# Two dense steps moved behind the corner products, and next block's keys released from the gate pair, in a hybrid RWKV-7 / short-convolution step

## The chip, the core and the metric

The kernel runs on one core of a Trainium2 chip, in one launch. The metric is the device time of that launch in microseconds (us). TensorE is PE in the profile (its weight loads are PEld), VectorE is DVE, ScalarE is ACT, GpSimd is POOL, and SP is the queue that issues nearly all the transfers. Each engine works through its own instructions in the order in which they stand in the program, and waits for others by semaphores.

## The reference

One layer of a diffusion backbone on 384 tokens (128 of a prompt, 256 of a sample), D = 2048. What matters here:

```python
z = h @ w_in                                   # one wide projection
zs = token_shift(z[..., :N_SHIFTED])           # r, k, v, low-rank decay and rate inputs
g_a, b_gate, c_gate, x_b, g_b, m_a, m_b = split(z[..., N_SHIFTED:])
decay = exp(-exp(-softplus(-w_lin) - 0.5)); a = sigmoid(...)
kk = k * k_k; kk = kk / max(norm(kk per head), 1e-12)
k_dir = k * (1 + (a - 1) * k_a)
# scan over tokens, both directions, 32 heads of 64:
S = S * w_t + (S @ (-kk_t)) outer (kk_t * a_t) + v_t outer k_t;  y = S @ r_t
y_a = (groupnorm(y) + bonus) * silu(g_a) @ w_out_a
y_b = (b_gate * conv3(c_gate * x_b) * silu(g_b)) @ w_out_b
out = x + gate * ((sigmoid(m_a) * y_a + sigmoid(m_b) * y_b) @ w_o)
```

Everything is float32. A dense product is made of three products of rounded parts (high by high, high by low, low by high).

## The kernel before

**Dense stream.** The wide projections are a stream of pairs: a pair is two output tiles of 128 columns, contracted over 2048, in 32 *dense steps* of three matmuls (L81, L82, L83) of 128x384. Its weights come in two halves; each half is loaded (`raw`), then split in two quarters by ACT (`whi`, L88) and DVE (`wlo`, L89). There are two `raw` buffers, and three each of `whi` and `wlo`. A generator gives out one dense step at a time: `ds_.go(n)` puts n of them on PE. TensorE's order is this written order; the other engines' order is set by a scheduler at build time from its own estimate and from priorities (the scan has a higher one).

**Scans.** 16 blocks of 128 channels (two heads) run one after the other, and their short products are put between dense steps. A block b runs:

- `prep_b`: scaled keys, the products `pA` (L695), masked into `A` by DVE (L701) for two directions. The 32x32 triangles on the diagonal of `A` are inverted on DVE: a chain of 60 small operations on `U` (L716, L718), ahead of it a trip through DRAM (`ui`), behind it a copy of the transpose on ACT (`UT`, L722), a second trip through DRAM (`uo`), and loads into `A` and `x11` (called x in the profile).
- `prep_c`: transposes, `pav`, the state.
- `prep_a(b + 1)`: the **keys of the next block**. Four low-rank products `pl` (weights `lraw`, split into `lwh` on ACT and `lwl` on DVE), a norm product `pn` (L633, L634), and then the key rows on DVE: `kn` (L636, three reciprocals L638, L639), `L` (L646), `kd` (L651, L652), `sig` (L653); the scheduler also puts rows of the next `prep_b` and `prep_c` behind them (`bk` L667 and L668, L775, L776).
- `scan`: the two **corner products** `pH` and `pX` (L843), each with four copies from PSUM, two on ACT and two on DVE in turn (L849 into x, L863 into `A`), three dense steps and the product `po` between them (with its addition L806 on DVE), then the **first solve** `pq` (L822), and the two chains of solves and state updates.

Block b needs its own rk pair (`rk{b}`: r and k) before `prep_a(b)`; the pair `gv{b}` gives block b's output gate and block b+1's v. At the start of each block the pairs `rk{b+1}` and `gv{b}` are put at the head of the stream; three filling pairs (tags ma, mb, bc, bx, bg, gb) follow. The dense steps between the parts are a table of numbers: H0 = 3 after `pH` and after `po`, H1 = 4 after `pX`, WINDOW = 80 from the end of `prep_b` to the scan.

The driver lets `prep_a(b + 1)` begin once `gv{b}` is done, and then fills up to the window. In blocks 2 to 14 the pair ends so late that `prep_a` stands directly ahead of `pH`, and the 80 steps are exceeded (84).

Of the kernel before, what the change touches and what calls it, by code (L numbers as in the profile page):

```python
# [20 lines left out]
NB = 16  # L21
# [35 lines left out]
def hybrid_step(ctx, tc, cst, x_prompt, x_sample, state_f, state_b, c, c_ctx, ada_w, ada_b, norm_g,  # L57
# [22 lines left out]
    def mm3(out, wh, wl, xh, xl, start, stop):  # L80
        TE.matmul(out, wh, xh, start=start, stop=False)  # L81
        TE.matmul(out, wh, xl, start=False, stop=False)  # L82
        TE.matmul(out, wl, xh, start=False, stop=stop)  # L83

    def split(src, shape, th, tl, pool, nm, rows=P):
        hi = pool.tile(shape, F32R, tag=th, name=f"{th}_{nm}")
        lo = pool.tile(shape, F32R, tag=tl, name=f"{tl}_{nm}")
        S.copy(hi[0:rows], src)  # L88
        V.tensor_tensor(lo[0:rows], src, hi[0:rows].bitcast(F32), ALU.subtract)  # L89
        return hi, lo  # L90


    PB0, PB1, H0, H1, CH0, CH1 = 14, 6, 3, 4, 2, 4
    PRO, WINDOW, FIRST, LAST = 32, 80, 24, 16

    def wload(view, k0, cols, nm):

# [84 lines left out]
    ds_ = Stream()  # L182
# [70 lines left out]
    def pcol(i, n=1):  # L253
        return par[:, i:i + n]
# [146 lines left out]
    r_, k_, v_, ga_ = {}, {}, {}, {}  # L401
    box = {}

    def tmp(nm):
        return box["sp"].tile([P, T], F32, tag="t", name=nm, bufs=8)
# [184 lines left out]
    def bank(nm):  # L590
        return ps1.tile([P, 4, P], F32, tag="A", name=nm, bufs=5)

    def c3(a):
        return a.rearrange("p (n t) -> p n t", t=C)

    def flat(a):
        return a.rearrange("p n t -> p (n t)")
# [4 lines left out]
    def hl_parts(t, hi, nm):  # L602
        lo = sp.tile([P, T], F32R, tag="t", name=f"lo_{nm}", bufs=8)
        S.copy(hi[:], t[:])
        V.tensor_tensor(lo[:], t[:], hi[:].bitcast(F32), ALU.subtract)
        return hi, lo

    def prep_a(b, o):

        bs = slice(b * P, (b + 1) * P)  # L610
        r, k, v = r_[b], k_[b], v_[b]
        kk = sp.tile([P, T], F32, tag="kk", name=f"kk_{b}")
        S.mul(kk[:], k[:], pcol(KK + b))
        sq = tmp(f"sq_{b}")
        S.activation(sq[:], kk[:], AF.Square)
        sqh, sql = hl_parts(sq, sp.tile([P, T], F32R, tag="hl", name=f"sqh_{b}"), f"sq_{b}")
        sig = []
        for m in range(4):
            if m % 2 == 0:
                lraw = sp.tile([96, 2, P], F32, tag="lraw", name=f"lraw_{b}_{m}")  # L620
                nc.sync.dma_start(lraw[:], (w2, a2)[m // 2][0][:, :, bs].rearrange("d r n -> r d n"))
                lwh, lwl = split(lraw[:], [96, 2, P], "lwh", "lwl", sp, f"{b}_{m}", rows=96)
                yield 2
            pl = bank(f"pl_{b}_{m}")
            pl = flat(pl[:, 0:3, :])
            mm3(pl, lwh[:, m % 2, :], lwl[:, m % 2, :], l_hi[:, m, :], l_lo[:, m, :], True, True)
            t = tmp(f"sig_{b}_{m}")
            S.activation(t[:], pl, AF.Sigmoid, bias=pcol((W0, W0 + 16, A0, A0 + 16)[m] + b))
            sig.append(t)
            yield 2  # L630
        pn = bank(f"pn_{b}")
        pn = flat(pn[:, 0:3, :])
        TE.matmul(pn, bones_r[:], sqh[:], start=True, stop=False)  # L633
        TE.matmul(pn, bones_r[:], sql[:], start=False, stop=True)  # L634
        kn = sp.tile([P, T], F32, tag="kn", name=f"kn_{b}")
        V.tensor_scalar(kn[:], pn, 1e-24, None, ALU.max)  # L636
        for q in range(3):
            V.reciprocal(kn[:, q * P:(q + 1) * P], kn[:, q * P:(q + 1) * P])  # L638
        V.scalar_tensor_tensor(kn[:], kk[:], -1.0, kn[:], ALU.mult, ALU.mult)  # L639
        o.update(kk=kk, ep=[], em=[], kd=[], bn=[])  # L640
        for d in range(2):
            def nat(a):
                return a[:, ::-1] if d else a[:]
            sg, aa = sig[d], sig[2 + d]
            L = tmp(f"L_{b}_{d}")
            V.tensor_tensor_scan(L[:], segm, sg[:], 0.0, op0=ALU.mult, op1=ALU.add)  # L646
            ep = eps_[b % 2, d]
            S.activation(ep[:, :, 1:C + 1], c3(L[:]), AF.Exp, scale=-DECAY)
            S.activation(sg[:], L[:], AF.Exp, scale=DECAY)
            kd = tmp(f"kd_{b}_{d}")  # L650
            V.tensor_scalar(kd[:], aa[:], pcol(KA + b), omka[:, b:b + 1], ALU.mult, ALU.add)  # L651
            V.tensor_tensor(kd[:], nat(k), kd[:], ALU.mult)  # L652
            V.tensor_tensor(aa[:], nat(kn), aa[:], ALU.mult)  # L653
            o["ep"].append(ep)
            o["em"].append(sg)
            o["kd"].append(kd)
            o["bn"].append(aa)
# [238 lines left out]
    def norm(b, o):  # L896

        ytok = o["ytok"]
        y6 = ytok[:].rearrange("p q (h i) -> p (q h) i", i=C)
        mu = sp.tile([P, 6], F32, tag="mu", name=f"mu_{b}")  # L900
        V.tensor_reduce(mu[:], y6, AX.X, ALU.add)
        V.tensor_scalar(mu[:], mu[:], 1.0 / C, None, ALU.mult)
        V.tensor_tensor(y6, y6, mu[:].unsqueeze(2).broadcast_to([P, 6, C]), ALU.subtract)
        sq = tmp(f"ysq_{b}")
        S.activation(sq[:], flat(ytok[:]), AF.Square)
        var = sp.tile([P, 6], F32, tag="var", name=f"var_{b}")
        V.tensor_reduce(var[:], sq[:].rearrange("p (q i) -> p q i", i=C), AX.X, ALU.add)
        V.tensor_scalar(var[:], var[:], 1.0 / C, GN_EPS, ALU.mult, ALU.add)  # L908
        rs = sp.tile([P, 6], F32, tag="rs", name=f"rs_{b}")
        G.tensor_tensor(rs[:], var[:], nhalf[:], ALU.pow)  # L910
        V.tensor_tensor(y6, y6, rs[:].unsqueeze(2).broadcast_to([P, 6, C]), ALU.mult)

    def finish(b, o):

        py = bank(f"py_{b}")
        for q in range(3):
            TE.transpose(py[:, q, :], o["ytok"][:, q, :], ident)
        ya = tmp(f"ya_{b}")
        S.activation(ya[:], flat(py[:, 0:3, :]), AF.Identity, scale=pcol(LG + b), bias=pcol(LB + b))
        V.tensor_tensor(ya[:], ya[:], o["bon"][:], ALU.add)  # L920
        V.tensor_tensor(ya[:], ya[:], ga_[b][:], ALU.mult)
        nc.sync.dma_start(ya_d[b], ya[:])

    def drive(gen, prio=0):
        n = 0
        while True:
            with tc.high_priority(offset=prio):
                u = next(gen, None)
            if u is None:
                return n  # L930
            ds_.go(u)
            n += u

    ds_.go(PRO)
    cur = {}
    drive(prep_a(0, cur))
    prev = None
    for b in range(NB):
        if b < NB - 1:
            if b > 0:  # L940
                ds_.urgent += [(add_rk, b + 1), (add_gv, b)]
        if b == NB - 2:
            ds_.fills += [(add_gv, NB - 1)] + [(add_ob, g) for g in range(8)]
        pb_gen = prep_b(b, cur)
        ds_.go(next(pb_gen))
        if prev is not None:
            finish(b - 1, prev)
        drive(pb_gen)
        n = drive(prep_c(b, cur))
        nxt = {}  # L950
        if b < NB - 1:
            while f"gv{b}" not in ds_.done:
                ds_.go(1)
                n += 1
            n += drive(prep_a(b + 1, nxt))
        w = WINDOW + (FIRST if b == 0 else LAST if b == NB - 1 else 0)
        if n < w:
            ds_.go(w - n)
        drive(scan(b, cur), 300)
        norm(b, cur)  # L960
        prev, cur = cur, nxt
# [97 lines left out]
    for nq in range(3):  # L1059
# [8 lines left out]
        for q in range(4):  # L1068
            raw = wp.tile([P, 4, 512], F32, tag="raw", name=f"raw_wo{nq}_{q}", bufs=2)
            nc.sync.dma_start(raw[:], wov[:, 4 * q:4 * q + 4, ns])  # L1070
            for e in range(2):
                hi, lo = split(raw[:, 2 * e:2 * e + 2, :], [P, 2, 512], "whi", "wlo", wp, f"wo{nq}_{q}_{e}")
                for s in range(3):
                    tsl = slice(s * P, (s + 1) * P)
                    for kk in range(2):
                        k = 4 * q + 2 * e + kk
# [7 lines left out]
    for half in range(2):  # L1084
# [8 lines left out]
        for s in range(3):  # L1093
# [10 lines left out]
            if half == 1:  # L1104
                f = rsf[:, s, :]
# [37 lines left out]
```

## Time and profile before

| what | value |
|---|---|
| time, median of 3 runs (lowest, highest) | 2264.56 us (2261.35, 2266.23) |
| the profiled execution: time, span | 2259.46 us, 2257.7 us |
| granted TensorE clock | 0.996 |
| busy: PE, DVE, ACT, POOL | 2187.7 us (97%), 1522.4 (67%), 1048.9 (46%), 118.6 (5%) |
| matmuls | 16084 |
| one block of the scans | about 106 us |

The time counts the launch as a whole, the span runs from the first instruction to the last; 1.8 us lie between them. A busy share is a mean over parts of the program with different limits. In the chain of work that ended last PE has 90%.

In the profile's rows, `x48` is a count, `out<-in` names tiles without their buffer numbers, a number in brackets is the idle time of that engine just before the row, with what ended it; "issue" means that the profile does not show what did.

### The profile page before, as it was taken

To read this page: it belongs to the slowest core of one execution; us is meant where nothing else is said; L and a number is where in the kernel's file an instruction comes from. 1 tells how busy PE (TensorE), PEld (TensorE's weight loads), DVE (VectorE), ACT (ScalarE), POOL (GpSimd) and SP (SyncE) were. 2 spreads that over 40 slices of the span, in tenths; PEclk is the share of its full clock that TensorE was granted. 3 is DMA by queue.
4 is the path that set the end of the run, shared out by engine and by line. 5 is a ranking of instruction groups with operands and counts; after the bars stand their busy time and mean duration, and the time that the engine had idled before them with its cause. 6 is when DMAs were issued, how large, how long until landed. Compare 5 with 4: busy or idle time off the path is not lost.

```text
span 2257.7 us, 40435 instructions
## 1 busy us (share of the span) xinstructions
PE 2187.7 (97%) x16084; PEld 2072.2 (92%) x16084; DVE 1522.4 (67%) x3096; ACT 1048.9 (46%) x1852; POOL 118.6 (5%) x115
## 2 busy tenths in 40 slices
PE   5999999999999999999999999999999999999998
PEld 3588999999999999999999999999999899889988
DVE  3249567777777778776878687777767774444444
ACT  4246445454545455454545454545455543333233
POOL 2001010101010100000010101010100000000000
PEclk9999999999999999999999999999999999999999
DMA  9963544444444444353444444444445465985633
GB/s 334 347 203 116 147 137 126 114 121 114 110 132 112 125 116 126 105 132 102 122 108 132 111 112 127 113 115 141 121 118 143 133 187 161 309 299 190 219 131 113
DMA packets 429646, 339.97 MB, mean 151 GB/s; under 512 B 84801, under 2 KB 411025, under 8 KB 428561
## 3 DMA queue, kind: packets, MB, share of 16 engines
q1 hardware_dynamic: 427968, 335.62, 50.6%
q8 instruction: 127, 2.08, 0.4%
q10 hardware_dynamic: 432, 1.57, 0.2%
q14 instruction: 63, 0.51, 0.1%
q0 software_dynamic: 1056, 0.19, 0.1%
HBM read 307.37 MB, written 29.36 MB: 149 GB/s over the span
## 4 chain that ended last, share of the span: by engine, by line
PE 90%; DMA 5%; DVE 2%; issue 2%; SPq 1%; ACT 1%; POOLq 0%; POOL 0%; DVEq 0%; ACTq 0%
PE d_rk L81 4%; PE d_gv L81 4%; PE d_gv L83 4%; PE d_gv L82 4%; PE d_rk L83 4%; PE d_rk L82 4%; DMA raw_adah<-in_ada_w_dram 3%; PE d_oa L81 2%; PE d_bx L81 2%; PE d_bg L81 2%; PE d_bc L81 2%; PE d_mb L81 2%; PE pq L822 2%; PE d_bg L83 2%; PE d_bg L82 2%; PE d_bx L83 2%
## 5 line engine op out<-in xcount | busy, mean ns | idle before, releaser
L716 DVE TENSOR_TENSOR ut<-U 48x30 f32<-48x30 f32 (+14 forms) x480 | 154.6, 322 | 16.2 <-DMA U<-ui 4.2
L81 PE MATMUL d_rk<-h_hi,whi_rk 128*128 128x384 f32 x480 | 164.3, 342 | 0.6 <-ACT lst L549 0.6
L718 DVE TENSOR_TENSOR U<-U,ut 48x30 f32<-48x30 f32 (+14 forms) x480 | 154.3, 321 | 10.8
L81 PE MATMUL d_gv<-h_hi,whi_gv 128*128 128x384 f32 x480 | 161.1, 336 | 0.0
L83 PE MATMUL d_gv<-h_hi,wlo_gv 128*128 128x384 f32 x480 | 160.8, 335 | 0.0
L82 PE MATMUL d_gv<-h_lo,whi_gv 128*128 128x384 f32 x480 | 160.7, 335 | 0.0
L83 PE MATMUL d_rk<-h_hi,wlo_rk 128*128 128x384 f32 x480 | 160.5, 334 | 0.0
L82 PE MATMUL d_rk<-h_lo,whi_rk 128*128 128x384 f32 x480 | 160.5, 334 | 0.0
L88 ACT CAST whi_gv<-raw_gv 128x1024 fp32r<-128x1024 f32 (+1 forms) x64 | 64.0, 999 | 141.1 <-PE d_rk L82 93.9
L89 DVE TENSOR_TENSOR wlo_rk<-raw_rk,whi_rk 128x1024 fp32r<-128x1024 f32 x60 | 72.9, 1218 | 44.6 <-ACT whi_rk L88 35.5
L88 ACT CAST whi_rk<-raw_rk 128x1024 fp32r<-128x1024 f32 x60 | 63.0, 1053 | 78.7 <-PE d_bx L82 16.4
L910 POOL TENSOR_TENSOR rs<-var,nhalf 128x6 f32<-128x6 f32 x16 | 21.2, 1326 | 1370.2 <-DVE var L908 1370.2
L81 PE MATMUL d_bg<-h_hi,whi_bg 128*128 128x384 f32 x256 | 92.8, 363 | 0.0
L81 PE MATMUL d_gb<-h_hi,whi_gb 128*128 128x384 f32 x256 | 92.5, 361 | 0.0
L81 PE MATMUL d_bc<-h_hi,whi_bc 128*128 128x384 f32 x256 | 92.4, 361 | 0.0
L81 PE MATMUL d_bx<-h_hi,whi_bx 128*128 128x384 f32 x256 | 92.3, 361 | 0.0
L81 PE MATMUL d_ma<-h_hi,whi_ma 128*128 128x384 f32 x256 | 92.0, 359 | 0.0
L81 PEld LDWEIGHTS d_rk<-h_hi,whi_rk 128*128 128x128 f32 x480 | 90.1, 188 | 1.8 <-ACT lst L549 0.9
L81 PEld LDWEIGHTS d_gv<-h_hi,whi_gv 128*128 128x128 f32 x480 | 90.5, 189 | 0.2
L81 PE MATMUL d_mb<-h_hi,whi_mb 128*128 128x384 f32 x256 | 90.6, 354 | 0.0
L82 PEld LDWEIGHTS d_gv<-h_lo,whi_gv 128*128 128x128 f32 x480 | 90.4, 188 | 0.0
L83 PEld LDWEIGHTS d_gv<-h_hi,wlo_gv 128*128 128x128 f32 x480 | 90.4, 188 | 0.0
(320 smaller groups left out, 6649.5 us busy)
## 6 DMA issues: line engine op xcount, KB each, us to landing
raw_adah<-in_ada_w_dram SPq DMA_DIRECT2D x64, 512.0 KB, 8.7
raw_rk<-in_w_in_dram SPq DMA_DIRECT2D x60, 512.0 KB, 5.3
raw_gv<-in_w_in_dram SPq DMA_DIRECT2D x60, 512.0 KB, 5.0
raw_ma<-in_w_in_dram SPq DMA_DIRECT2D x16, 1024.0 KB, 5.5
raw_mb<-in_w_in_dram SPq DMA_DIRECT2D x16, 1024.0 KB, 5.4
raw_bc<-in_w_in_dram SPq DMA_DIRECT2D x16, 1024.0 KB, 5.6
raw_bx<-in_w_in_dram SPq DMA_DIRECT2D x16, 1024.0 KB, 5.5
raw_bg<-in_w_in_dram SPq DMA_DIRECT2D x16, 1024.0 KB, 5.4
```

Source lines behind the costliest of these rows:

```text
L81: TE.matmul(out, wh, xh, start=start, stop=False)
L82: TE.matmul(out, wh, xl, start=False, stop=False)
L83: TE.matmul(out, wl, xh, start=False, stop=stop)
L88: S.copy(hi[0:rows], src)
L89: V.tensor_tensor(lo[0:rows], src, hi[0:rows].bitcast(F32), ALU.subtract)
L716: V.tensor_tensor(tv, U[:, 0:s, s:s + 1].broadcast_to([48, s, w]), U[:, s:s + 1, s + 1:].broadcast_to([48, s, w]), ALU.mult)
L718: V.tensor_tensor(U[:, 0:s, s + 1:], U[:, 0:s, s + 1:], tv, ALU.add)
L822: TE.matmul(pq[:, d, :], A[:, 0, f, :], sav[:, f, :], start=True, stop=True)
L910: G.tensor_tensor(rs[:], var[:], nhalf[:], ALU.pow)
```

## The change

H1 goes from 4 to 6: two more dense steps between `pX` and the first `pq`. The window goes from 80 (84 in effect) to 79 with the 12 steps of `prep_a` in it, so that there are two fewer ahead of `pH`. `prep_a(b + 1)` now needs `rk{b+1}` to be done and no longer `gv{b}`; it always stands directly ahead of the scan, in block 0 too. `finish(b - 1)` makes sure that the gate pair is done. H1's name in the code is in the table of numbers; the number of dense steps in all and every computed value stay the same.

```diff
-    PB0, PB1, H0, H1, CH0, CH1 = 14, 6, 3, 4, 2, 4
-    PRO, WINDOW, FIRST, LAST = 32, 80, 24, 16
+    PB0, PB1, H0, H1, CH0, CH1 = 14, 6, 3, 6, 2, 4
+    PRO, WINDOW, FIRST, LAST, PA = 32, 79, 16, 16, 12
...
     def prep_a(b, o):
         bs = slice(b * P, (b + 1) * P)
-        r, k, v = r_[b], k_[b], v_[b]
+        k = k_[b]
...
         if prev is not None:
+            ds_.until(f"gv{b - 1}")
             finish(b - 1, prev)
         drive(pb_gen)
         n = drive(prep_c(b, cur))
         nxt = {}
         if b < NB - 1:
-            while f"gv{b}" not in ds_.done:
+            while f"rk{b + 1}" not in ds_.done:
                 ds_.go(1)
                 n += 1
-            n += drive(prep_a(b + 1, nxt))
         w = WINDOW + (FIRST if b == 0 else LAST if b == NB - 1 else 0)
+        if b < NB - 1:
+            w -= PA
         if n < w:
             ds_.go(w - n)
+        if b < NB - 1:
+            drive(prep_a(b + 1, nxt))
         drive(scan(b, cur), 300)
```

On PE, counted in dense steps from the end of `prep_c` (its product `psi`), a block from 2 to 14 had the first `pl` at 62, `pn` and `pH` at 72, `pX` at 78 and `pq` at 82; now these stand at 60, 70, 76 and 82. The pair `gv{b}` ended two steps ahead of the first `pl`, and now ends eleven steps ahead of it. A block is 160 dense steps, which are five pairs, in both kernels.

The other engines' order follows from the scheduler. On DVE, around the corner products of block 5 before, from the reciprocals of the next block's keys to the first copy out of `pX` (this order, with other numbers, is also that of blocks 3, 7, 9, 11, 13 and 14):

```order
L638 RECIPROCAL kn_7968<-kn_7968 128x128 x2
L849 COPY x_5_7504<-pH_7991 32x6x32
L638 RECIPROCAL kn_7968<-kn_7968 128x128
L849 COPY x_5_7504<-pH_7991 32x6x32
L639 SCALAR_TENSOR_TENSOR kn_7968<-kk_7873,kn_7968 128x384
L806 TENSOR_TENSOR sav_7515<-po_1_0_8029,sav_7515 64x2x128
L652 TENSOR_TENSOR kd_0_7978<-k_7735,kd_0_7978 128x384
L653 TENSOR_TENSOR sig_2_7945<-kn_7968,sig_2_7945 128x384
L646 SCALAR_TENSOR_TENSOR L_1_7982<-cs,sig_1_7921 128x384
L859 TENSOR_TENSOR bon_8060<-pbn_8057,v_6721 128x384
L89 TENSOR_TENSOR wlo_bc_0_0_8044<-raw_bc_0_8041,whi_bc_0_0_8043 128x1024
L863 COPY A_7342<-pX_8062 32x6x32
```

Now, in block 5 (block 9 has the same), up to the two copies out of `pH`; ahead of the first row stand `kn` L636, `kd` L651, the reciprocals x3, `kd` L652, `kn` L639 and `L` L646:

```order
L653 TENSOR_TENSOR sig_2_7862<-kn_7885,sig_2_7862 128x384
L668 TENSOR_TENSOR bk_0_8329<-kd_0_7895,sig_0_7816 128x6x64
L667 TENSOR_TENSOR bk_0_8329<-sig_2_7862,sig_0_7816 128x6x64
L651 TENSOR_SCALAR kd_1_7903<-sig_3_7874,par,omka 128x384
L89 TENSOR_TENSOR lwl_0_8943<-lraw_0_8940,lwh_0_8942 96x256
L652 TENSOR_TENSOR kd_1_7903<-k_7615,kd_1_7903 128x384
L653 TENSOR_TENSOR sig_3_7874<-kn_7885,sig_3_7874 128x384
L668 TENSOR_TENSOR bk_1_8335<-kd_1_7903,sig_1_7828 128x6x64
L667 TENSOR_TENSOR bk_1_8335<-sig_3_7874,sig_1_7828 128x6x64
L775 TENSOR_TENSOR kd_0_7895<-kd_0_7895,kd_1_7903 128x384
L776 SCALAR_TENSOR_TENSOR kd_0_7895<-kd_0_7895,par,r_7595 128x384
L849 COPY x_5_7432<-pH_7908 32x6x32 x2
```

The two copies have moved from among the reciprocals to behind the whole set of key rows. In block 3 (7 and 11 have the same) they have moved part of that way:

```order
L638 RECIPROCAL kn_5589<-kn_5589 128x128 x3
L652 TENSOR_TENSOR kd_0_5599<-k_5319,kd_0_5599 128x384
L639 SCALAR_TENSOR_TENSOR kn_5589<-kk_5496,kn_5589 128x384
L646 SCALAR_TENSOR_TENSOR L_1_5603<-cs,sig_1_5532 128x384
L653 TENSOR_TENSOR sig_2_5566<-kn_5589,sig_2_5566 128x384
L668 TENSOR_TENSOR bk_0_6039<-kd_0_5599,sig_0_5520 128x6x64
L667 TENSOR_TENSOR bk_0_6039<-sig_2_5566,sig_0_5520 128x6x64
L849 COPY x_3_5136<-pH_5612 32x6x32
L651 TENSOR_SCALAR kd_1_5607<-sig_3_5578,par,omka 128x384
L89 TENSOR_TENSOR lwl_0_6651<-lraw_0_6648,lwh_0_6650 96x256
L849 COPY x_3_5136<-pH_5612 32x6x32
```

The first copy now stands behind six more rows, and two rows stand between the copies. In block 4, on DVE, the order before (also that of blocks 1, 8 and 12) was:

```order
L638 RECIPROCAL kn_6824<-kn_6824 128x128
L849 COPY x_4_6352<-pH_6847 32x6x32
L638 RECIPROCAL kn_6824<-kn_6824 128x128
L806 TENSOR_TENSOR sav_6363<-po_1_0_6885,sav_6363 64x2x128
L849 COPY x_4_6352<-pH_6847 32x6x32
```

and it is now, in block 4 and likewise in blocks 0, 1, 2, 6, 8, 10, 12, 13 and 14:

```order
L638 RECIPROCAL kn_6733<-kn_6733 128x128
L849 COPY x_4_6280<-pH_6756 32x6x32
L638 RECIPROCAL kn_6733<-kn_6733 128x128
L806 TENSOR_TENSOR sav_6291<-po_1_0_6794,sav_6291 64x2x128
L89 TENSOR_TENSOR wlo_bc_0_1_6700<-raw_bc_0_6693,whi_bc_0_1_6699 128x1024
L849 COPY x_4_6280<-pH_6756 32x6x32
```

One weight split (`wlo`) has come between the addition L806 and the second copy.

## The prediction

> **What bounds the kernel now.** I read the page first, then the waits of PE, then the timeline of PE and DVE around the corner products.
>
> ```profile
> span 2257.7 us, 40435 instructions
> PE 2187.7 (97%) x16084; PEld 2072.2 (92%) x16084; DVE 1522.4 (67%) x3096; ACT 1048.9 (46%) x1852; POOL 118.6 (5%) x115
> ```
>
> PE works 2187.7 of 2257.7 us, so its 70 us of idle time are all that an edit of the order can win or enlarge: no product is added or taken away. The waits of PE, with total, count and longest:
>
> ```profile
> PE pq L822 <- issue: 16.6, 10, 2.0
> PE pX L843 <- issue: 1.1, 1, 1.1
> ```
>
> The first solve `pq` waits in ten of the sixteen blocks, 16.6 us in all, and `pX` once. That is 17.7 us around the corner products, the sum that the change can take away. Whom they wait for shows in block 3: first PE, with two matmuls of block 5 that are one dense step apart (0.52 us) as the last rows, then DVE.
>
> ```profile
> 583.37 0.34 PE L634 MATMUL pn<-lo_sq,bones_r 128*128 128x384 f32 x1
> 583.64 0.62 PE L843 MATMUL pH<-x,A 32*32 32x32 f32 x48
> 588.34 0.62 PE L843 MATMUL pX<-A,x 32*32 32x32 f32 x48
> 593.02 0.68 PE L822 MATMUL pq<-sav,A 128*128 128x128 f32 x4 [1.78 <-issue]
> ...
> 801.25 0.34 PE L81 MATMUL d_gb<-h_hi,whi_gb 128*128 128x384 f32 x1
> 801.77 0.33 PE L81 MATMUL d_gb<-h_hi,whi_gb 128*128 128x384 f32 x1
> ```
>
> ```profile
> 583.75 0.56 DVE L636 TENSOR_SCALAR kn<-pn 128x384 f32<-128x384 f32 x1 [0.54 <-PE pn L634]
> 584.22 0.47 DVE L651 TENSOR_SCALAR kd<-sig,par,omka 128x384 f32<-128x384 f32 x1
> 584.61 1.76 DVE L638 RECIPROCAL kn<-kn 128x128 f32<-128x128 f32 x2
> 586.39 0.35 DVE L849 COPY x<-pH 32x192 f32<-32x192 f32 x1
> 586.78 0.95 DVE L638 RECIPROCAL kn<-kn 128x128 f32<-128x128 f32 x1
> 587.76 0.36 DVE L849 COPY x<-pH 32x192 f32<-32x192 f32 x1
> 588.15 0.56 DVE L639 SCALAR_TENSOR_TENSOR kn<-kk,kn 128x384 f32<-128x384 f32 x1
> 588.74 0.42 DVE L806 TENSOR_TENSOR sav<-po,sav 64x256 f32<-64x256 f32 x1
> 589.08 0.54 DVE L652 TENSOR_TENSOR kd<-k,kd 128x384 f32<-128x384 f32 x1
> 589.55 0.54 DVE L653 TENSOR_TENSOR sig<-kn,sig 128x384 f32<-128x384 f32 x1
> 590.02 0.94 DVE L646 TENSOR_TENSOR_SCAN L<-cs,sig 128x384 f32<-128x384 f32 x1
> 590.88 0.52 DVE L859 TENSOR_TENSOR bon<-pbn,v 128x384 f32<-128x384 f32 x1
> 591.33 1.21 DVE L89 TENSOR_TENSOR wlo_bg<-raw_bg,whi_bg 128x1024 fp32r<-128x1024 f32 x1
> 592.57 0.35 DVE L863 COPY A<-pX 32x192 f32<-32x192 f32 x1
> ```
>
> From the first key row (583.75, which waits for `pn`) DVE runs back to back. It reaches the first copy into `A` at 592.57 and ends it at 592.92; `pq` starts at 593.02. PE was ready at 591.24. So "issue" is DVE: the corner products are a race from `pn`, between PE's short stretch of dense steps and a queue of key rows with the copies somewhere in it. On one clock that starts at 583.75: PE is at `pX` at +4.59 and at `pq` at +7.49; the copies out of `pH` end at +2.99 and +4.37, in time, and the copy for `pq` at +9.17, late.
>
> **The two moved steps alone.** From `pX` to `pq` PE now has 2.90 + 2 x 0.52 = 3.94 us instead of 2.90. With DVE's old order a wait of 1.78 would fall to 0.74, so at ten waits to some 7 us. That order is gone, though, and the copies have to be counted anew, in the order shown ahead, with the durations of the trace: start to start in the rows above, and for the others these.
>
> ```profile
> 470.18 0.41 DVE L89 TENSOR_TENSOR lwl<-lraw,lwh 96x256 fp32r<-96x256 f32 x1
> ...
> 490.75 0.62 DVE L776 SCALAR_TENSOR_TENSOR kd<-kd,par,r 128x384 f32<-128x384 f32 x1
> ...
> 595.01 0.54 DVE L668 TENSOR_TENSOR bk<-kd,sig 128x384 f32<-128x384 f32 x1
> 595.48 0.54 DVE L667 TENSOR_TENSOR bk<-sig,sig 128x384 f32<-128x384 f32 x1
> ```
>
> **Blocks 5 and 9.** Ahead of the copies out of `pH` now stand 0.47 (L636), 0.39 (L651), 3 x 0.89 (reciprocals), 0.47 (L652), 0.59 (L639), 0.86 (L646), 0.47 (L653), 2 x 0.47 (L668, L667): 6.86 us; then 0.39, 0.41 (`lwl`), 2 x 0.47, 2 x 0.47, 0.47 (L775, taken like L668) and 0.62: 10.6 us. The two copies end at 10.6 + 0.38 + 0.36 = +11.4. `pX` reads x in the order of its four parts and is due at +4.59, so PE waits 6.8 us in its first matmuls. It does not matter where PE is with `pH`: L636 reads `pn`, and all this is queued behind it. After `pX` there are L806, one `wlo`, `bon` and the copy into `A`, 0.34 + 1.24 + 0.45 + 0.35 = 2.4 us against PE's 3.94: no wait at `pq`. Two blocks: 13.6 us.
>
> **Blocks 3, 7 and 11.** The first copy starts behind the 6.86 us, the second behind 0.38 + 0.39 + 0.41 more, and ends at +8.4. `pX` waits 3.8 us. Then L652, L806, `wlo`, L653, `bon`, L667 and the copy take 0.47 + 0.34 + 1.24 + 0.47 + 0.45 + 0.47 + 0.35 = 3.8 against 3.94: nothing at `pq`, by a hair. Three blocks: 11.4 us.
>
> **The other ten blocks** (0, 1, 2, 4, 6, 8, 10, 12, 13, 14) get what block 4 had, plus a `wlo`:
>
> ```profile
> 690.37 0.56 DVE L636 TENSOR_SCALAR kn<-pn 128x384 f32<-128x384 f32 x1 [0.53 <-PE pn L634]
> ...
> 693.58 0.42 DVE L806 TENSOR_TENSOR sav<-po,sav 64x256 f32<-64x256 f32 x1
> 694.02 0.36 DVE L849 COPY x<-pH 32x192 f32<-32x192 f32 x1
> ...
> 694.96 0.62 PE L843 MATMUL pX<-A,x 32*32 32x32 f32 x48
> ...
> 697.70 0.60 PE L822 MATMUL pq<-sav,A 128*128 128x128 f32 x4
> ```
>
> Block 4 had no wait: the second copy ended at 694.38, `pX` started at 694.96. With 1.21 of `wlo` ahead of it the copy ends at 695.6, 0.6 us after `pX` is due. `pq` is then safe. Ten blocks: 6.0 us. Here the change does what it says.
>
> **Ahead of `pn`.** The triangle chain ends with the `UT` copy on ACT, and DVE's copies of v and gate, with more weight splits, now fall into the chain instead of behind it, because `gv` ends nine steps earlier. Relevant is not `pH` but the third `pl`, whose weights ACT and DVE split behind `UT`:
>
> ```profile
> 571.02 2.09 ACT L722 COPY UT<-U 48x1024 f32<-48x1024 f32 x1 [3.52 <-DVE U L718]
> ...
> 580.01 0.34 PE L81 MATMUL pl<-l_hi,lwh 96*128 96x384 f32 x1
> ```
>
> From the end of `UT` (573.11) to this `pl` were 6.9 us. Two dense steps fewer leave 5.9. In blocks 5 and 9 the chain takes in two more `wlo`, `ga`, four rows of v and `lo_sq`, less one row: I estimate 4.5 us from rows like those above, and some 3 us for filling rows and a `wlo` ahead of the masks that start it. That overdraws the 5.9 by 1.6, and the split behind `UT` takes another 1.4: 3.0 us of wait. In blocks 3, 7 and 11 the same count gives 1.6, in the ten others 0.5. The sum is 2 x 3.0 + 3 x 1.6 + 10 x 0.5 = 15.8, the upper bound; the lower is 0, since ACT and DVE have idle time there that may take it up. No row is near enough to choose, so I take half, 8.
>
> **Costed at nothing.** The dense steps are the same in number, and what a scan does not use is done after the last block. `finish` waits for a gate pair that ended in the block before. ACT loads its function table 47 times instead of 33 in the built order, beside `pq`; ACT is busy for 46%, and a table that comes ahead of the copies out of `pq` would cost at most some tenths in six blocks. On SP, the loads of x behind `uo` have at most one other load ahead of them, as before; should they land later in five blocks, by my count DVE's copies are later still. Block 15 has no keys to prepare, and its rows move by fractions of a us.
>
> **A price beside this.** After the wait of 1.97 us ahead of `pq` in block 2 the granted clock was 0.50 for 3.4 us:
>
> ```profile
> 486.30:489.70 3.40, 3.40 (x15) 3.40 (x14) 3.12 (x6) 1.57 (x3) 0.00 (x0) 0.50 0.00 0
> ```
>
> That costs half of it, 1.7 us. It is one of ten such waits, so for five waits of 3.8 to 6.8 us I take 0, with 5 x 1.7 = 8.5 as the upper bound. [...]
>
> **Sum.** 13.6 + 11.4 + 6.0 = 31.0 at `pX`, 8 ahead of `pn`, less 17.7: **+21.3 us**. The profiled execution would go from 2259.46 (span 2257.7 and 1.8 around it) to 2280.8. The median of the runs, 2264.56, lies 5.1 above that execution; to it the sum gives **2286**.
>
> **Rivals.**
> - *The waits vanish and the copies cost little: faster.* It is one mechanism, DVE getting through the key rows ahead of the copies faster than I count, in five blocks. If nothing were left there, 2264.56 - 17.7 + 6 = 2253. The point of balance is a mean wait of (17.7 - 6.0) / 5 = 2.3 us in those five blocks, against my mean of 5.0. For it: a row of DVE often starts before the one ahead has ended. Against: I used distances of starts, and L636 cannot start before `pn`. 0.08.
> - *As much is lost as won: no change, 2265.* DVE would have to be twice as fast there, or pieces of the wait fall together with other idle time of PE; there is hardly any. 0.09.
> - *The late chain and the clock at their upper bounds: slower still.* -17.7 + 31.0 + 15.8 + 8.5 gives +37.6, 2302. For it: `pl` has no slack left by my count. 0.20.
> - *The change does not do what it says: `pq` still waits.* In blocks 3, 7 and 11 the margin is 0.1 us, so up to 1 us in three blocks; it lies inside the range.
>
> **How the numbers follow.** My forecast has 0.63, with its own range of 2276 to 2295 (from 0 to 15.8 ahead of `pn`). A difference of 0.2%, 4.5 us, is about what a measurement of this kernel can tell from no change. The range that leaves out no more than 2 in 10 goes from the case of no change, 2265, to 2303. Faster by over 0.2% 0.08, within 0.09, slower 0.83.
>
> **What would show it.** In the waits of PE: `pq` gone or under 2 us in all; `pX` with about 15 waits, 31 us in all, the longest two near 6.8 us, three near 3.8, ten near 0.6, ended by "issue" or by DVE's L849. On DVE in block 5, L849 behind L776, with no idle time ahead of it. Waits of `pl` for `lwh` or `lwl` between 0 and 16 us. Stretches at 0.5 of the clock behind the longest waits. I am wrong if `pX` waits under 2.3 us in blocks 3, 5, 7, 9 and 11, or if PE waits before `pn` for longer than 16 us.

## The result, and the profile after

The changed kernel took 2271.05 us (median of 10 runs, 2267.53 to 2275.07), the kernel before 2264.82 us in the runs beside it: a ratio of 1.0028 with a 95% interval of 1.0018 to 1.0038. It is slower by 6.2 us, where 21.3 were forecast. Timed once more later, beside other runs of before, it stood at 2274.24 against 2264.69, ratio 1.0038 (1.0025 to 1.0051). Its profiled execution took 2273.07 us, 13.6 more than that of before; so the two profiles are further apart than the medians, and that has to be explained too.

The page of the changed kernel, span and busy times:

```profile
span 2271.3 us, 40401 instructions
PE 2199.1 (97%) x16084; PEld 2084.1 (92%) x16084; DVE 1522.5 (67%) x3096; ACT 1068.7 (47%) x1866; POOL 121.5 (5%) x115
```

PE's idle time rose by only 2.2 us, from 70.0 to 72.2. The same 16084 matmuls took 11.4 us longer. That is the first thing to see: the loss looks like slow matmuls, not like waits. The waits of PE in the changed kernel (total, count, longest):

```profile
PE pH L843 <- DMA x<-uo: 13.9, 10, 2.3
PE pX L843 <- DVE x L849: 4.8, 13, 1.0
PE pl L81 <- ACT lwh L88: 4.2, 3, 1.4
PE pv L750 <- DVE A L701: 3.0, 2, 2.3
```

`pq` has gone from the list, as forecast. But `pX` waits 4.8 us and not 31, and never over 1.0 us, where the prediction had named waits under 2.3 us in the five blocks as a sign of being wrong. The largest wait is one step earlier, ahead of `pH`, for the loads of x. Now DVE, then PE, in block 5:

```profile
785.27 0.56 DVE L636 TENSOR_SCALAR kn<-pn 128x384 f32<-128x384 f32 x1 [0.91 <-PE pn L634]
...
794.93 0.62 DVE L776 SCALAR_TENSOR_TENSOR kd<-kd,par,r 128x384 f32<-128x384 f32 x1
795.58 0.35 DVE L849 COPY x<-pH 32x192 f32<-32x192 f32 x1
796.31 0.36 DVE L849 COPY x<-pH 32x192 f32<-32x192 f32 x1 [0.38 <-ACT x L849]
```

```profile
781.34 0.45 PE L81 MATMUL pl<-l_hi,lwh 96*128 96x384 f32 x1 [1.42 <-ACT lwh L88]
...
786.89 0.39 PE L843 MATMUL pH<-x,A 32*32 32x32 f32 x24 [1.65 <-DMA x<-uo]
788.56 0.55 PE L843 MATMUL pH<-x,A 32*32 32x32 f32 x24 [1.28 <-DMA x<-uo]
...
789.52 0.52 PE L82 MATMUL d_bg<-h_lo,whi_bg 128*128 128x384 f32 x1
789.84 0.52 PE L83 MATMUL d_bg<-h_hi,wlo_bg 128*128 128x384 f32 x1
...
795.63 0.94 PE L843 MATMUL pX<-A,x 32*32 32x32 f32 x6
796.72 0.57 PE L843 MATMUL pX<-A,x 32*32 32x32 f32 x42 [0.15 <-DVE x L849]
```

From the first key row to the end of the second copy are 796.67 - 785.27 = 11.40 us, and 11.4 were forecast; in block 3 it was 8.17 (576.54 + 0.36 - 568.73) against 8.4. DVE's queue was counted right to 0.3 us; that block 5 agrees more closely than that is luck, since the first copy started 0.3 us earlier than counted and the second then waited 0.38 us for ACT. PE, due at `pX` 4.6 us after the first key row, came 10.4 us after it: 2.93 us went in the two waits ahead of `pH`, and then its matmuls took 0.32 us from start to start instead of 0.175. Block 3, first on DVE, then on ACT and PE:

```profile
568.73 0.56 DVE L636 TENSOR_SCALAR kn<-pn 128x384 f32<-128x384 f32 x1 [1.05 <-PE pn L634]
...
576.54 0.36 DVE L849 COPY x<-pH 32x192 f32<-32x192 f32 x1
```

```profile
559.29 2.12 ACT L722 COPY UT<-U 48x1024 f32<-48x1024 f32 x1 [1.35 <-DVE U L718]
...
568.36 0.34 PE L634 MATMUL pn<-lo_sq,bones_r 128*128 128x384 f32 x1
...
577.55 0.62 PE L843 MATMUL pX<-A,x 32*32 32x32 f32 x48
```

Here PE came to `pX` 8.82 us after the first key row, 0.65 us behind the end of the last copy on DVE, and did not wait at all; in blocks 7 and 11 it came 0.9 and 2.4 us behind that copy. So in these three blocks DVE's late copies did not set the time: PE was later still, by its waits for x (2.4 to 2.8 us a block) and its slow matmuls. The loads of x follow on the triangle chain, and that chain ends late: `UT` ended 7.3 us ahead of the end of `pn` here and 4.7 us in block 5, where it was 10.6 us in both blocks before. The prediction had counted this lateness, and had priced it at the third `pl`; most of it shows at `pH`.

The granted clock behind the long waits of blocks 3, 5 and 11 (blocks 7 and 9 had 3.4 us each):

```profile
572.55:575.97 3.42, 3.42 (x14) 3.42 (x13) 3.35 (x8) 1.90 (x5) 0.00 (x0) 0.50 0.02 5
787.59:794.42 6.83, 5.86 (x42) 5.80 (x43) 6.83 (x15) 1.25 (x3) 0.00 (x0) 0.50 0.09 22
...
1439.54:1446.37 6.83, 6.56 (x44) 6.50 (x45) 6.67 (x14) 3.51 (x8) 0.00 (x0) 0.50 0.06 17
```

The third number from the end, 0.50, is the granted clock (behind it stand the share of the transfers and GB/s; ahead of it the busy times of PE, weight loads, DVE, ACT and POOL). Five such stretches, 23.9 us in all, cost PE about 12 us (an estimate, half of their length). They lie between the first key row and `pX`, while DVE works through its queue, so in blocks 5 and 9 they took the place of the wait at `pX` and did not come on top of it; `first_20` below shows this with and without such a stretch.

**Where the time lies.** A block is taken here from the end of its last `pA` matmul to that of the next; blocks 2 to 14 have 823 matmuls each in both kernels, and an undisturbed one takes 104.55 us (block 4 of before). The views of three stretches (blocks 0 and 1; blocks 2 to 14; all behind that), each with length, PE's busy time, clock, transfers; first before, then the changed kernel, each in its first profile:

```profile
194.50:423.30 228.80, 228.57 (x1760) 1.00 0.47 134
423.30:1808.60 1385.30, 1365.67 (x10700) 1.00 0.44 120
1808.60:2257.70 449.10, 436.50 (x2666) 0.99 0.61 200
```

```profile
193.70:412.80 219.10, 218.17 (x1697) 1.00 0.47 134
412.80:1812.00 1399.20, 1375.14 (x10702) 0.99 0.42 117
1812.00:2271.30 459.30, 448.56 (x2731) 0.99 0.62 205
```

The thirteen blocks lose 13.9 us. Blocks 0 and 1 win 9.7, since 63 matmuls (21 dense steps) fewer stand there; the last stretch has them more and is 10.2 us longer. The time over 104.55 us, by groups of blocks:

| kernel | eight other blocks, mean | blocks 3, 7, 11 | blocks 5, 9 | thirteen blocks |
|---|---|---|---|---|
| before | 1.9 | 2.1, 2.0, 2.0 | 2.1, 2.5 | 26.1 |
| changed | 0.6 | 4.2, 4.4, 5.9 | 9.4, 11.0 | 40.0 |

### The profile page after: what moved, and what is told of

The parts are those of the page before. It is cut to its first block, busy times and chain, and to the rows that moved or that the text cites. A ratio compares the mean times of both kernels' runs of the same rounds, so it can differ in the third digit from the quotient of the medians.

```text
span 2271.3 us, 40401 instructions
## 1 busy us (share of the span) xinstructions
PE 2199.1 (97%) x16084; PEld 2084.1 (92%) x16084; DVE 1522.5 (67%) x3096; ACT 1068.7 (47%) x1866; POOL 121.5 (5%) x115
## 4 chain that ended last, share of the span: by engine, by line
PE 84%; DVE 6%; DMA 6%; ACT 1%; issue 1%; SPq 1%; POOLq 0%; POOL 0%; DVEq 0%; ACTq 0%
PE d_rk L81 4%; PE d_gv L81 3%; PE d_gv L82 3%; DMA raw_adah<-in_ada_w_dram 3%; PE d_gv L83 3%; PE d_rk L83 3%; PE d_rk L82 3%; PE d_oa L81 2%; PE d_bc L81 2%; PE d_oa L83 2%; PE d_oa L82 2%; PE d_mb L81 2%; PE d_gb L81 2%; PE d_bc L82 2%; PE d_bc L83 2%; PE d_mb L83 2%
## 5 line engine op out<-in xcount | busy, mean ns | idle before, releaser
L81 PE MATMUL d_rk<-h_hi,whi_rk 128*128 128x384 f32 x480 | 172.2, 359 | 0.6 <-ACT lst L549 0.6
L718 DVE TENSOR_TENSOR U<-U,ut 48x30 f32<-48x30 f32 (+14 forms) x480 | 154.5, 322 | 10.8
L89 DVE TENSOR_TENSOR wlo_oa<-raw_oa,whi_oa 128x1024 fp32r<-128x1024 f32 x32 | 39.2, 1224 | 78.3 <-ACT whi_oa L88 78.3
L82 PEld LDWEIGHTS d_rk<-h_lo,whi_rk 128*128 128x128 f32 x480 | 90.6, 189 | 0.0
L824 ACT COPY sav<-pq 64x128 f32<-64x128 f32 x192 | 50.4, 262 | 85.3 <-PE pq L822 83.0
```

Of the source, the lines that this page charges most:

```text
L718: V.tensor_tensor(U[:, 0:s, s + 1:], U[:, 0:s, s + 1:], tv, ALU.add)
L824: S.copy(sav[0:C, fs, hss[h]], pq[hss[h], 0:2, hss[h]])
```

## The experiments

Theory A, as in the prediction: the order of DVE's rows decides, and the time of a block follows from when the copies out of `pH` and into `A` come in that order. Against it stand rivals that each run names.

**Both kernels once more.** No edit; new profiles and runs.

> The kernel before, unchanged, profiled once more and timed. Theory A (the count of waits was right for the profiled execution, and the median carries half-rate stretches of the clock that this one execution had been spared): the profiled execution of before had a mean granted clock of 0.996 and one half-rate stretch in the scans; here the runs, near 2265 us, show 0.993 to 0.994, about 2.3 us for each 0.001, and a profile near 2265 us shows three to five half-rate stretches of 3.4 us behind the waits of 1.6 to 2.0 us ahead of pq. The waits themselves stay at 16 to 18 us in all. Rival B (the 5.1 us between that execution and the median lie elsewhere, in transfers or the start): the clock is 0.996 in every run, whatever its time, and the new profile has other waits.

Measured: 2263.81 us (ratio to before 0.9999, 0.999 to 1.0008), clocks of 0.991 to 0.995 in eleven runs. The profiled execution took 2266.32 us at 0.992, 6.9 more than the first one, with the same waits:

```profile
PE pq L822 <- issue: 17.7, 10, 2.0
```

and two more half-rate stretches in the scans, behind `pq` of blocks 7 and 11 (rows 2 and 3 below; the first is that behind block 2, as in the first profile), and two in the last stretch:

```profile
485.67:489.08 3.41, 3.41 (x14) 3.41 (x13) 3.19 (x6) 1.57 (x3) 0.00 (x0) 0.50 0.00 0
1018.15:1021.56 3.41, 3.41 (x14) 3.41 (x14) 3.16 (x6) 1.77 (x4) 0.00 (x0) 0.50 0.00 0
1444.81:1448.23 3.42, 3.42 (x14) 3.42 (x13) 2.70 (x5) 1.57 (x3) 0.00 (x0) 0.50 0.03 7
1816.87:1820.28 3.41, 3.41 (x13) 3.24 (x14) 3.41 (x7) 2.58 (x6) 0.00 (x0) 0.50 1.02 336
1946.57:1953.40 6.83, 6.19 (x20) 6.10 (x20) 6.21 (x10) 3.48 (x6) 0.00 (x0) 0.50 0.78 245
```

Blocks 7 and 11 took 3.6 us over 104.55 instead of 2.0, at waits of 1.80 and 1.81 us, nearly the 1.78 of the first profile. The same wait brings a half-rate stretch in one execution and none in the next. Over the 28 runs of before that stand beside the later experiments the mean clock was 0.9942, and the time fell by 1.5 us for each 0.001 (a straight line through them, where 2.3 us were expected; the clock explains it only in part). The execution that the prediction was made from had 0.996. Theory A holds, with a smaller slope; B fell.

> The changed kernel, unchanged, profiled once more and timed. Median 2271 us. Theory A: the five long waits (2.4 to 5 us of standing PE in blocks 3, 5, 7, 9 and 11) bring half-rate stretches in nearly every execution: five or six stretches in the scans, 17 to 27 us long in all, and mean clocks of 0.990 to 0.993. Block by block the time over the undisturbed 104.55 us is 0.5 to 0.8 in ten blocks, 4 to 6 in blocks 3, 7 and 11, 9 to 11 in blocks 5 and 9, as in the first profile (40 us in all). Rival B: these excesses move between blocks from one execution to the next by several us, so that no block's own wait explains them.

Measured: 2274.24 us (the ratio above), clocks 0.989 to 0.992; the eight blocks again at 0.6, blocks 3, 7, 11 at 3.9, 5.8, 4.5, blocks 5 and 9 at 13.4 and 11.2, 43.8 in all. The losses stay in their blocks, with block 5 above its range by 2.4 us. `pX` waits more here, 8.2 us and up to 2.8 us, and x less, 11.6 us. Half rate in the scans was 34.1 us long, above the 17 to 27 expected; half of the 10.2 us more than in the first profile would be 5.1 us, and the blocks grew by 3.8.

**The two parts of the change, each alone.**

```
order_alone   (on before):  H0, H1 = 3, 4 -> 3, 6     WINDOW 80 -> 78
release_alone (on after):   H0, H1 = 3, 6 -> 3, 4     WINDOW 79 -> 81
```

> One part alone: the kernel before with two dense steps moved from ahead of the corner products to between these and pq (H1 6, WINDOW 78); the next keys still wait for the gate and v pair. By the count of DVE rows ahead of the second copy out of pH (3.8 to 8.0 us from the first key row, PE due at 4.6): pq's 16.6 us of waits go, pX waits 0.7 us in eight blocks, 3.0 to 3.4 us in blocks 4, 8 and 12, and 0.2 in two, 15 us in all. Theory A: so 2258 to 2266 us, with the half-rate stretches now behind blocks 4, 8 and 12 alone. Rival C (the moved steps only win, and what the whole change loses comes from releasing the next keys): pq's waits go and none come, 2245 to 2250 us.

Measured: 2275.80 us, ratio 1.0053 (1.0039 to 1.0066): slower than the whole change, and neither expectation was right. Its clock was 0.994, as before. In blocks 2 to 14 PE waited

```profile
PE pq L822 <- issue: 8.2, 9, 1.0
PE pX L843 <- DVE x L849: 4.1, 12, 0.4
PE pH L843 <- DMA x<-uo: 3.9, 5, 1.4
```

`pX` waits 0.4 us in most blocks, near the expected 0.7; the miss is `pq`, which still waits nine times, up to 1.0 us. My expectation counted the order only up to `pX`. In the trace the first copy into `A` ends 10.0 us after the first key row in the eight blocks where `pq` waits 0.95 us or more, 0.4 to 0.9 us later than in before, and PE is due there at 8.5 + 0.4. Two steps take 1.04 us of a wait of 1.6 to 2.0, and the new order gives a good part of that back. Blocks 4, 8 and 12 lose most, 4.6, 4.7 and 4.0 us over 104.55, but not as expected in waits of 3.0 to 3.4 us at `pX` alone: part of it is the wait for x, 1.0 to 1.4 us, and in block 4 a half-rate stretch. Thirteen blocks: 36.8 us. On PE this kernel has, from block 2 on, the dense steps of the changed one (`pX` at 76, `pq` at 82), and yet it loses in other blocks; so PE's own steps do not decide which blocks lose.

> The other part alone: the changed kernel with the two dense steps back ahead of the corner products (H1 4, WINDOW 81); the next keys wait only for their own rows, as in the change. By the count of DVE rows: the second copy out of pH ends 8.7 us after the first key row in blocks 3, 7 and 11 and 12 us in blocks 5 and 9, PE due at 4.6, and 3.8 us in the ten others, where nothing is then lost. Theory A: pq's waits are gone by the release alone (under 3 us in all), the five blocks lose 4 to 6 and 9 to 11 us as in the changed kernel, the other ten are at 104.6 to 105 instead of 105.2, so 2265 to 2273 us, at most 5 us below the changed kernel. Rival C: the release alone loses what the change loses and leaves pq's waits too: 2285 us or more.

Measured: 2275.10 us, ratio 1.0048 (1.0036 to 1.0061), clock 0.991. `pq` is gone from the waits by the release alone, and the blocks are those of the change: 7.1, 4.4, 4.4 in 3, 7 and 11, 12.1 and 12.3 in 5 and 9, 0.7 in the eight others, 45.7 in all. `pX` waits 10.8 us here, up to 2.3 us. Theory A, at 2 us above its upper end; C fell. Each part alone costs some 11 us, and both together 6 to 10: they do not add up, and each edit makes a new order of DVE's rows.

**The copies out of `pH` all on ACT.**

```
-  (S.copy, V.tensor_copy)[j % 2](x11[32:64, j::4, :], pz[j])
+  S.copy(x11[32:64, j::4, :], pz[j])
```

> The changed kernel with all four copies out of pH on ACT, which holds no key rows there; transfers and dense steps as in the changed kernel. Theory A (DVE's key rows set the end in blocks 3, 5, 7, 9 and 11, and PE's own waits and its half rate ahead of that only fill the time): the waits for x<-uo ahead of pH stay (2.4 to 2.9 us), pX waits no more, and the copy into A, still behind the key rows, ends 11.7 to 13 us after the first one, so pq waits 1 to 2 us in the five blocks; blocks 5 and 9 fall from 9 to 13 us of excess to 5 to 7, blocks 3, 7 and 11 from 4 to 6 to about 3, the ten others from 0.7 to 0.2: 2252 to 2261 us. Rival B (the late x<-uo and the half rate behind it set the end, DVE's order only follows): the five blocks stay as they are, and only the ten others gain, some 5 us: 2265 to 2270 us.

Measured: 2259.45 us, ratio to before 0.9982 (0.9973 to 0.9991), some 11 us below the changed kernel by the ratios. The eight blocks went from 0.6 to 0.1, blocks 5 and 9 from 9.4 to 13.4 down to 7.0 and 7.1, blocks 3, 7 and 11 only from 3.9 to 5.9 to 4.1, 4.5 and 3.8. The wait ahead of `pH` stayed:

```profile
PE pH L843 <- DMA x<-uo: 12.1, 10, 2.3
```

The sum is inside A's range, but not for A's reason everywhere. `pq` was to wait 1 to 2 us in each of the five blocks for the copy into `A`, which still stands behind the key rows, and it waited once, 0.55 us in block 11. In the others the wait for x and a half-rate stretch brought PE to `pq` just behind that copy: 12.76 us after the first key row in block 5, where the copy ended at 12.66, and 12.46 against 11.98 in block 3. So two causes of nearly the same length run side by side there, and this run does not tell them apart. It does show what it saves to take the copies out of `pH` from DVE: some 0.6 us in each short block, as counted, 2.4 to 6.4 us in 5 and 9 (6.8 counted), and a mean of 0.7 us in 3, 7 and 11 (3.8 counted).

**The loads of x ahead of those of A.**

```
+  for d in range(2):
+      nc.sync.dma_start(x11[0:32, 12 * d:12 * d + 12, :], uo[1, d, 0]...)
   for d in range(2):
       for e in range(2):
           nc.sync.dma_start(blocks(A, d, e), uo[0, d, e]...)
-      nc.sync.dma_start(x11[0:32, 12 * d:12 * d + 12, :], uo[1, d, 0]...)
```

> The changed kernel with the two loads of x from uo issued ahead of the four loads of A (program order; nothing else). In the order built from it blocks 3, 7 and 11 then have the copies among the reciprocals (second copy ends 3.4 us after the first key row instead of 8), blocks 5 and 9 end theirs at 9.0 to 9.4 instead of 10.8 to 11.2, the others are as they were. Theory A: blocks 3, 7 and 11 keep only a wait for x<-uo of 0 to 1 us, blocks 5 and 9 lose 6 to 7 us (4.6 at pX, 1.4 ahead of pn), the rest 0.7: 22 us of excess instead of 40 to 44, 2248 to 2256 us. Rival B (only the landing counts): blocks 5 and 9 too fall to 2 to 3 us, 2243 to 2247 us. If the queue of transfers and not the order of the issues decides when x lands, nothing changes: 2271 us.

Measured: 2257.76 us, ratio to before 0.9979 (0.9969 to 0.9989; one of twelve runs, at 7590.22 us, is no part of the ratio). In the profile, an execution 7 us above the median, blocks 3, 7 and 11 fell to 1.6, 3.8 and 3.3, blocks 5 and 9 stayed at 10.3 and 10.4 (6 to 7 expected). The thirteen blocks kept 34.7 us where 22 were expected. Theory A in its direction, 2 us above its range; B fell, since 5 and 9 did not go to 3. In 3, 7 and 11 DVE's copies now end 3.9 to 4.8 us after the first key row and PE comes to `pX` behind them, so what is left there is the wait for x and the half rate: block 3 had a wait of 1.1 us and no half-rate stretch, block 11 a wait of 1.2 us and one stretch of 3.4 us.

**Another phase.** Only the steps of block 0 change, and with them which products every later block meets.

```
first_14:  PRO, WINDOW, FIRST, LAST, PA = 32, 79, 16, 16, 12 -> 32, 79, 14, 16, 12
first_20:                                                    -> 32, 79, 20, 16, 12
```

> The changed kernel with one number other: FIRST 14 instead of 16, so that block 0 takes two dense steps fewer ahead of its scan and every later block meets the row of dense products two steps earlier in its turn. Theory A (the loss of the changed kernel is DVE's key rows standing ahead of the copies out of pH, in the blocks where the order built puts them so): in the order of this kernel the second copy ends 4.7 us after the first key row in every block (PE due at 4.6) and the first copy into A 7.8 us after it (pq due at 8.5). So no block waits more than 0.5 us, the time over 104.55 us falls from 40 to 44 us in thirteen blocks to 2 to 6, hardly any half-rate stretches are left in the scans, and the time is 2232 to 2242 us. Rival C (the release of the next keys or the moved steps cost in themselves, in every turn): 2260 us or more.

> The changed kernel with FIRST 20 instead of 16: another phase. In its order the second copy out of pH ends 9.3 to 9.7 us after the first key row in every block (due at 4.6), the first copy into A 3.6 to 4.1 us behind it (3.94 us between pX and pq). Theory A: every block is like blocks 3, 7 and 11 or a little worse, 5 to 7 us of excess with the half rate that such waits brought there, 65 to 90 us in thirteen blocks instead of 40 to 44: 2293 to 2318 us. Rival D (a wait of this kind is mostly made good by other idle time, as the small net loss of the change suggests): under 2285 us.

Measured: FIRST 14 took 2261.13 us (ratio 0.9987, 0.9978 to 0.9996), FIRST 20 took 2315.71 us (1.0230, 1.0212 to 1.0248). So one number in block 0 moves the changed kernel by 55 us, and which blocks lose is decided there. FIRST 20 is in A's range, with 73.9 us in thirteen blocks and all of them at 5 to 7. Its waits in blocks 2 to 14:

```profile
PE pH L843 <- DMA x<-uo: 25.5, 26, 1.5
PE pX L843 <- DVE x L849: 4.9, 13, 0.4
PE pX L843 <- ACT x L849: 4.0, 4, 1.9
```

Again PE loses more ahead of `pH` than at `pX`, and the blocks last about as long as DVE's queue: its second copy ends 9.5 us after the first key row in twelve of the thirteen blocks, 4.9 us behind the 4.6 at which PE is due. These blocks also show what half rate costs here. Blocks 3, 7 and 11 have their copies at the same times after the first key row. Blocks 3 and 11 have a stretch of 3.4 us at half rate between that row and `pX`, and block 7 has none. Block 3, then block 7:

```profile
590.85 0.97 PE L843 MATMUL pX<-A,x 32*32 32x32 f32 x6
...
1031.91 0.97 PE L843 MATMUL pX<-A,x 32*32 32x32 f32 x6 [1.86 <-ACT x L849]
```

In both, `pX` starts 8.16 us after the first key row, in block 7 with a wait of 1.86 us ahead of it and in block 3 without. The blocks took 5.44 us (3 and 11) and 5.60 us (7) over 104.55: under DVE's queue the half rate cost nothing that shows.

FIRST 14 missed: 27.6 us instead of 2 to 6, in a time that rival C had named. Block 4 shows where A's count fell short, DVE first.

```profile
680.57 0.53 DVE L636 TENSOR_SCALAR kn<-pn 128x384 f32<-128x384 f32 x1
...
685.01 0.36 DVE L849 COPY x<-pH 32x192 f32<-32x192 f32 x1
```

```profile
684.61 0.26 PE L843 MATMUL pX<-A,x 32*32 32x32 f32 x6
685.43 0.57 PE L843 MATMUL pX<-A,x 32*32 32x32 f32 x42 [0.56 <-DVE x L849]
...
693.00 0.71 PE L829 MATMUL pu<-sav,bt 128*128 128x128 f32 x4 [0.67 <-ACT sav L824]
```

The copy ends 4.80 us after the first key row (4.7 counted), but that row itself starts late, behind another row of DVE, so that PE is at `pX` 4.0 us after it and not 4.6. And ACT has two table loads of 1.28 us ahead of its copies out of `pq`, for which `pu` waits up to 0.7 us in five blocks; the prediction had costed such loads at nothing, and in the changed kernel itself `pu` does not wait. These waits are about 1.2 us of the 1.9 us of block 4, and the rest is not accounted for. Rival C is settled only by the next runs.

**Both repairs, and the repair without the change.** `x_first_10` has the loads of x first and FIRST 10; `x_first_10_act` also the copies on ACT; `before_x_first` is the kernel before with the loads of x first and nothing else.

> Both together: loads of x first, and FIRST 10. In the order built every block ends the second copy 3.4 us after the first key row (due at 4.6) and the first copy into A at 6.8 to 7.3 (due at 8.5). Theory A: no waits around the corner products, excess of 0 to 3 us in thirteen blocks, 2230 to 2240 us, the fastest of all, 1 to 4 us below FIRST 14 alone. Rival C: 2260 us or more.

> The fastest so far (x first, FIRST 10: 2243.4 us, 9 us of excess left in thirteen blocks) with all four copies out of pH on ACT. In x_on_act that took 0.7 us from each block whose copies stood among the reciprocals. Here pX no longer waited, and what is left are waits of 0.2 to 0.6 us of pq, po and pu for the copies behind them. Theory A: DVE's copy into A ends at 7.0, as before, so nothing is won at pX; with 0.7 us less on DVE ahead of L806 the waits of pq for sav go (1.7 us): 2240 to 2243 us, not to be told from it. Rival E (ACT is late with its copies, since they stand behind its exponentials): pX waits 0.5 us or more in every block, 2250 us.

> The kernel before with nothing of the change, only the two loads of x from uo issued ahead of the four loads of A. In the order built from it every block has the copies among the reciprocals: the second copy out of pH ends 3.8 us after the first key row (PE due at 4.6), the first copy into A at 6.5 in seven blocks and 7.0 to 7.4 in six (pq due at 7.5). Theory A (DVE's order decides; each of the ten waits ahead of pq cost more than its length, 26 to 29 us of excess in thirteen blocks for 17.7 us of waiting): pq waits 0 to 0.5 us in six blocks and not in the others, the excess falls to 2 to 8 us, 2240 to 2247 us: as fast as the best version with the change. Rival B (the late landing of x sets the end and the order of DVE follows): the same gain only if pH waited before, which it did for 0.4 us in all; so 2262 us.

| kernel | median us | ratio to before (95%) | thirteen blocks over 104.55 |
|---|---|---|---|
| x_first_10 | 2243.35 | 0.9911 (0.9898 to 0.9924) | 9.2 |
| x_first_10_act | 2244.58 | 0.9917 (0.9904 to 0.9931) | 11.0 |
| before_x_first | 2242.36 | 0.9906 (0.9893 to 0.9920) | 6.3 |

All three beat both kernels by about 1%. With 2243.35 us, and the release and the two steps in it, rival C fell. Theory A held each time, with a miss in size: `x_first_10` lay 3 us above its range (9.2 us left instead of 0 to 3) and `x_first_10_act` 2 us above its own; ACT's copies bring nothing more. The third one matters most here: the kernel before had waited 0.4 us in all for x, yet the order of those loads took away nearly all of its waits ahead of `pq`, because DVE's rows were then built in another order: the first copy into `A` ends 6.8 to 7.7 us after the first key row, where in the waiting blocks of before it was 9.2 to 9.6. What is left of the waits in the scans:

```profile
PE pq L823 <- issue: 1.9, 6, 0.3
```

(L823 is the former L822.) `x_first_10` and `before_x_first` differ by the change itself and by FIRST, and not in time. So the change is worth nothing that these runs can tell, once DVE's order is good in both.

## Why the prediction was right in sign and wrong in size

The kernel with nearly none of these waits, `before_x_first`, gives a base for both terms:

```profile
423.80:1789.20 1365.40, 1361.83 (x10700) 1.00 0.44 122
```

Against these 1365.4 us for thirteen blocks (6.3 over undisturbed ones), before took 19.9 us more (22.6 in its second profile), and the changed kernel 33.8 (37.5).

- **Added: right in size, in part by luck.** For these blocks the forecast had 37.3 us (31.0 + 8, less 1.7 for blocks 0 and 1). Measured 33.8 and 37.5. The kinds too: 0.6 to 0.7 in the short blocks (0.85 forecast with the share ahead of `pn`), 3.9 to 5.9 in 3, 7 and 11 (4.6), 9.4 to 13.4 in 5 and 9 (8.3). The mechanism was right in the short blocks and in 5 and 9, where DVE's queue sets the time. In 3, 7 and 11 the wait for x and the half rate were by chance as long as DVE's queue. And the 8 us ahead of `pn` were 2.8 at `pl`; the half rate, taken at 0, filled the difference.
- **The place: wrong.** The wait that was to stand at `pX` (31 us) was 4.8, and 8.2 in the second profile. PE lost the time earlier, in the waits for x (13.9 and 11.6) and at half rate, while DVE's queue ran. The prediction had written that loads of x landing later cost nothing, since DVE is later still: for the time that was nearly right in blocks 5 and 9, where `pX` still waited for DVE's copies in both profiles (0.2 to 2.8 us), and wrong in 3, 7 and 11, where PE came to `pX` behind them.
- **Removed: this term was mis-sized.** "Less 17.7" priced a wait at its length. In the profiles it was 19.9 and 22.6; before_x_first, which took nearly all of these waits away, gained 21.9 us at the median. In blocks 2 to 13 a wait of 1.6 to 2.0 us cost the block 2.0 to 2.5 us over block 4, which has none, and 3.6 to 4.1 where a half-rate stretch followed, behind one of ten such waits in one execution and three of ten in the other. The prediction saw that stretch in block 2, and put its price on the new waits only, as an upper bound, and not on the old ones that the change removes.
- **"The median lies 5.1 above that execution; to it the sum gives 2286": this step failed too.** Those 5.1 us were taken as a constant. They were an execution spared of half-rate stretches: the clock 0.996 against a mean of 0.994. The second profile of before had 17.1 us more of half rate in the scans and the last stretch, which would be 8.5 us, and took 6.9 us longer. The changed kernel's execution lay 2.0 above its own median. Carrying the sum over as it was added about 7 us: 13.6 between the two executions, 6.2 between the medians.
- **Costed at nothing: the first blocks and the end.** The forecast had +1.7 there. The two pairs of profiles give +0.5 and -7.7 (the second: 228.7 and 453.8 us against 219.2 and 455.6). The 21 dense steps that moved to the end cover waits there (3.8 and 4.7 us in before, 2.1 and 0.4 after, among them those of the first steps of the output for their inputs); half rate differs there from one execution to the next as well, none and 10.2 us of it in the two profiles of before and 3.4 us and none after.

So of the 15.1 us that the forecast of 21.3 had too much, 7.4 were the step from the execution to the median, 5.7 the thirteen blocks (19.6 forecast, 13.9 measured; 3.5 of it added, 2.2 removed) and 2.0 the rest of the kernel. In the second pair of profiles the thirteen blocks took 14.9 us more and the ends 7.7 less; so the shares change with the executions, while the removed term was too small in both. Of the rivals none came true, but that of no change had named what happened: pieces of the wait fell together with other lost time of PE. The upper bounds (2302) were far off, since waits, half rate and DVE's queue lay over each other where they had been added up.

What half rate costs by itself, the traces show in part. Under DVE's queue it cost nothing that shows (`first_20`, and `order_alone`: block 4 with a stretch 4.6 us, block 8 without one 4.7). Where no queue covers it, a stretch of 3.4 us cost 1.6 to 1.7 us: 3.6 against 2.0 us in blocks 7 and 11 of before, 4.1 in block 2 against 2.4 in block 6, and 3.3 against 1.6 us in blocks 11 and 3 of x_first. What stays open is why some waits bring such a stretch and others of the same length do not, and how much of the loss in blocks 3, 7 and 11 of the changed kernel would be left if x landed in time and DVE's order stayed: x_first changed both.

## What to carry to other kernels

Where PE meets a queue of another engine, count that queue from the row that starts it: it was right to 0.3 us in both long kinds of block, whatever PE did in between, but it sets the time only where PE is not later still (for PE's side of the race the start of that row has to be counted too, which first_14 missed), and what PE lost within it (waits, slow matmuls) did not add up (in `first_20` 5.44 us a block with a half-rate stretch, 5.60 us without). Price a wait that an edit removes by a block that has it against one that has not, not by its length in the list. And when a scheduler builds the order, an edit of two steps, a number in the first block or the order of two loads can move the time by more than the edit is about: read the built order of each variant ahead of the rows, and try the phase first.

## What was not expected of the hardware

- A PE wait of 1.8 us was followed by 3.4 us at half clock in one execution and by none in the next, and waits of 1.7 to 2.3 us with a shorter one close behind by 3.4 or 6.8 us. The granted clock also differed between the runs of the same kernel: 0.991 to 0.996 in those of before, 0.989 to 0.993 in those of the changed kernel.
- Two loads of x issued ahead of four of A, on a queue that PE waited for 0.4 us in all, made the kernel 0.94% faster, as far as the waits show by way of the order that was built and not of the transfers.
